# A sparse 3x3 convolution on one core: a fifth pair of images loaded up front in two parts, a wait ahead of the first store, and twelve more matmuls on zeros

## The chip, the core and the metric

The kernel runs on one core of a Trainium2 chip. The core has five engines that run their own instruction streams: TensorE (PE in the profile, with its weight loads shown as PEld), VectorE (DVE), ScalarE (ACT), GpSimd (POOL) and SyncE (SP, which here only issues transfers). Sixteen DMA engines move data between the chip's memory (HBM) and the on-chip buffer (SBUF); matmuls write to the accumulators (PSUM). Engines wait for each other by semaphores.

The metric is the time of one execution on the device in microseconds (us); the median over several executions is given. A profiled execution also leaves a trace, in which the span from the first to the last instruction can be read engine by engine.

## The reference

A batch of 16 images with 64 channels of 64 x 64 is convolved with 128 filters of 3 x 3, padding 1. About 90% of the weights are zero, but the kernel treats them as any others.

```python
batch, c_in, h, w, c_out, k = 16, 64, 64, 64, 128, 3
x_pad = np.pad(x, ((0, 0), (0, 0), (pad, pad), (pad, pad)), mode='constant')
for b in range(batch):
    for co in range(c_out):
        for ci in range(c_in):
            for kh in range(k):
                for kw in range(k):
                    if weight[co, ci, kh, kw] != 0:
                        output[b, co] += weight[co, ci, kh, kw] * x_pad[b, ci, kh:kh+h, kw:kw+w]
```

Input and output are 32-bit floats: 16.8 MB of images are read and 33.6 MB of results are written.

## The kernel before

**Tiling.** Two images form a pair, `p` = 0 to 7. The 64 channels of the first image lie on partitions 0 to 63, those of the second on 64 to 127, in a bf16 tile `xs[p]` of 128 x 64 x 64 (`x0` to `x7`, all eight held at once). A matmul takes 64 partitions, one filter tap and 8 rows of 64 pixels, and the matmuls for the two images of a pair alternate, each on its half of the array. A pair is worked in four blocks of 16 rows.

**Two ways to compute a block.** Only the first block of pair 0 is done by `direct` (L150): nine taps, added up in PSUM, copied out by ScalarE and VectorE. All others are done by `twos` (L157), which saves products by working on two output rows at once: GpSimd adds neighbouring rows into `s` (L160), the products of `s` with the middle filter row are shared by even and odd output rows, ScalarE copies them to `pc` (L167), and VectorE adds `pc` to the products of the even and of the odd rows (L174), writing the output tile `o`. This needs differences of filter rows (`G21`, `G01`, L107), made once at the start.

**Start.** SyncE issues the load of the weights (L60) and of the upper 32 rows of pair 0 in 32-bit form (L62). GpSimd issues the lower half of pair 0 (L63), then the identity matrix for transposing, then the pairs 1 to 3 (L68, `EARLY = 4`). Transfers issued by GpSimd convert to bf16 on the way. They run in queue q0, those of SyncE in queue q1, and both queues are served by the same 16 DMA engines. Meanwhile TensorE runs 27 matmuls on a tile of zeros (L80), whose result nobody reads; then it transposes the three filter rows (L103), with casts before (L97) and copies behind them (L116 to L120). The upper half of pair 0 is cast in three pieces by VectorE and ScalarE (L93), and the products (L141) begin when the first piece is there.

**Order.** The schedule is written by hand (`manual_schedule`): each engine runs its instructions in the order of the program text. SyncE's queue holds the two loads of the start and then only stores: two per pair, each of one whole image (L198, 2 MB), issued once VectorE has written all of it; for the last pair four of 1 MB (L195). GpSimd's queue holds the adds (L160) and, between them, the loads of the later pairs: in pair `p`, block 1, it issues the load of pair `p + 3` (L187, L188), so pair 4 during pair 1. Output tiles come from a pool of seven buffers, of which the head of pair 0 uses one at first.

Of the kernel before, what the change touches and what calls it, by code (L numbers as in the profile page):

```python
# [27 lines left out]
def kernel(  # L28
# [6 lines left out]
    nc = tc.nc  # L35

    B, C_IN, H, W = x.shape
    C_OUT, _, KH, KW = weight.shape
    assert (B, C_IN, H, W) == (16, 64, 64, 64) and (C_OUT, KH, KW) == (128, 3, 3)
    NP = B // 2  # L40
# [14 lines left out]
    def pair(p):  # L55
        return x[2 * p : 2 * p + 2].rearrange("n i h w -> (n i) h w")

    xs = [x_pool.tile([128, H, W], BF16, name=f"x{p}") for p in range(NP)]
# [5 lines left out]
    ident = const_pool.tile([128, 128], BF16, name="ident")  # L64
    make_identity(nc, ident)

    def load(p):
        nc.gpsimd.dma_start(out=xs[p], in_=pair(p))  # L68


    EARLY = 4
    for p in range(1, EARLY):
        load(p)


    idle_rhs = const_pool.tile([128, 128], BF16, name="idle_rhs")
    nc.vector.memset(idle_rhs, 0.0)  # L77
    idle_ps = psum_pool.tile([128, 128], FP32, name="ps")
    for _ in range(27):
        nc.tensor.matmul(idle_ps, idle_rhs, idle_rhs, start=True, stop=True)  # L80

# [8 lines left out]
    def cast_x(copy, a, b):  # L92
        copy(out=xs[0][:, a:b, :], in_=x_head[:, a:b, :])  # L93
# [5 lines left out]
    def transposed(g):  # L99
        wps = psum_pool.tile([128, 4, 128], FP32, name="ps")  # L100
        for j in range(3):
            src = w_bf[:, g, C_IN * j : C_IN * (j + 2)]
            nc.tensor.matmul(wps[:, j, :], src, ident, start=True, stop=True)  # L103
        return wps[:, 0:3, :]

    def difference(g, wps):
        nc.vector.tensor_tensor(out=wT[:, g], in0=wps, in1=wT[:, G1], op=SUB)  # L107
# [10 lines left out]
    nc.vector.tensor_copy(out=wT[:, G0], in_=ps0)  # L118
    ps2 = transposed(G2)
    nc.scalar.copy(out=wT[:, G2], in_=ps2)  # L120
    cast_x(nc.scalar.copy, 9, 18)
    difference(G01, ps0)
    difference(G21, ps2)
# [26 lines left out]
    def direct(p, o, r0, rows):  # L150
        ps = product(
            [(xs[p], G1, r0, 1), (xs[p], G0, r0 - 1, 1), (xs[p], G2, r0 + 1, 1)], rows
        )
        nc.scalar.copy(out=o[0][:, r0 : r0 + rows, :], in_=ps[0])  # L154
        nc.vector.tensor_copy(out=o[1][:, r0 : r0 + rows, :], in_=ps[1])  # L155

    def twos(p, o, r0):  # L157
        t0 = r0 // 2
        s = s_pool.tile([128, 8, W], BF16, name="s")
        nc.gpsimd.tensor_tensor(  # L160
            out=s, in0=xs[p][:, r0 : r0 + 16 : 2, :], in1=xs[p][:, r0 + 1 : r0 + 16 : 2, :], op=ADD
        )
        shared = product([(s, G1, 0, 1)], 8)
        pc = []
        for n in range(2):
            c = p_pool.tile([128, 8, W], FP32, name="pc")
            nc.scalar.copy(out=c, in_=shared[n])  # L167
            pc.append(c)
        even = [(xs[p], G21, r0 + 1, 2), (xs[p], G0, r0 - 1, 2)]
        odd = [(xs[p], G01, r0, 2), (xs[p], G2, r0 + 2, 2)]  # L170
        for first, terms in ((r0, even), (r0 + 1, odd)):
            ps = product(terms, 8)
            for n in range(2):
                nc.vector.tensor_tensor(  # L174
                    out=o[n][:, first : r0 + 16 : 2, :], in0=ps[n], in1=pc[n], op=ADD
                )

    for p in range(NP):
        o = [o_pool.tile([C_OUT, H, W], FP32, name="o") for _ in range(2)]
        last = p == NP - 1  # L180
        for blk in range(4):
            r0 = 16 * blk
            if BLOCKS[p][blk] == "T":
                twos(p, o, r0)


                if p > 0 and blk == 1 and p + EARLY - 1 < NP:  # L187
                    load(p + EARLY - 1)  # L188
            else:
                for r, rows in ((r0, 8), (r0 + 8, 8)):  # L190
                    direct(p, o, r, rows)
            if last and blk % 2 == 1:
                for n in range(2):
                    rows = slice(r0 - 16, r0 + 16)
                    nc.sync.dma_start(out=out[2 * p + n][:, rows, :], in_=o[n][:, rows, :])  # L195
        if not last:
            for n in range(2):
                nc.sync.dma_start(out=out[2 * p + n], in_=o[n])  # L198


# [28 lines left out]
```

## Time and profile before

| what | value |
|---|---|
| median of 6 executions | 127.4 us (127.31 to 131.36) |
| the profiled execution's own time | 127.35 us |
| its span, first to last instruction | 125.5 us |
| TensorE busy | 108.6 us, 87% of the span |
| VectorE busy | 82.3 us, 66% |
| GpSimd busy | 40.6 us, 32% |
| ScalarE busy | 38.9 us, 31% |
| mean granted clock of TensorE | 0.952 of full speed |
| bytes moved, as the DMA engines count them | 42.93 MB, mean 342 GB/s |
| loads of 1 MB in bf16 by GpSimd, issue to landing | 15.6 us in the median |
| stores of 2 MB, issue to landing | 16.5 us in the median |

How to read it: a busy share is an average over the whole span. A transfer's "landing" is the time at which its completion is signalled, so it holds the time behind other transfers in its queue as well as its own. Bytes are counted as they are written: a casting load reads two bytes for each that it counts, so 210 GB/s of such loads and 420 GB/s of stores keep the DMA engines equally busy. The clock column of a window is the share of TensorE's full clock that was granted in it. A window is a stretch of the span in us, and its row gives the busy time of each engine with the number of instructions in brackets, then clock, DMA share and GB/s. "SPq" is SyncE's issuing of a transfer, "POOLq" GpSimd's.

### The profile page before, as it was taken

To read this page: it belongs to the slowest core of one execution; us is meant where nothing else is said; L and a number is where in the kernel's file an instruction comes from. 1 tells how busy PE (TensorE), PEld (TensorE's weight loads), DVE (VectorE), ACT (ScalarE), POOL (GpSimd) and SP (SyncE) were. 2 spreads that over 40 slices of the span, in tenths; PEclk is the share of its full clock that TensorE was granted. 3 is DMA by queue.
4 is the path that set the end of the run, shared out by engine and by line. 5 is a ranking of instruction groups with operands and counts; after the bars stand their busy time and mean duration, and the time that the engine had idled before them with its cause. 6 is when DMAs were issued, how large, how long until landed. Compare 5 with 4: busy or idle time off the path is not lost.

```text
span 125.5 us, 2486 instructions
## 1 busy us (share of the span) xinstructions
PE 108.6 (87%) x1002; PEld 55.8 (44%) x1002; DVE 82.3 (66%) x135; ACT 38.9 (31%) x71; POOL 40.6 (32%) x45
## 2 busy tenths in 40 slices
PE   6539999999999999999999999999999999990000
PEld 6414454554455455545555455545554554540000
DVE  0343278788878877877787778777877787774000
ACT  4541533333333333333333333333333333330000
POOL 6309434333433343334333333333333330000000
PEclk9977999999999999999999999999999999999655
DMA  4999999999999999999999999999999999999990
GB/s 135 348 230 212 217 209 217 214 151 402 444 358 303 319 386 363 319 324 379 379 295 313 379 423 428 439 428 415 433 433 423 433 413 418 428 420 407 426 384 37
DMA packets 4044, 42.93 MB, mean 342 GB/s; under 512 B 448, under 2 KB 448, under 8 KB 704
## 3 DMA queue, kind: packets, MB, share of 16 engines
q1 hardware_dynamic: 2880, 34.90, 66.2%
q0 software_dynamic: 1152, 7.86, 30.9%
q8 instruction: 8, 0.13, 0.4%
q14 instruction: 4, 0.03, 0.1%
HBM read 17.07 MB, written 33.55 MB: 403 GB/s over the span
## 4 chain that ended last, share of the span: by engine, by line
PE 82%; DMA 5%; DVE 1%; issue 1%; DVEq 0%; SPq 0%
PE ps L141 82%; DMA o<-in_x_dram 5%; DVE o L174 1%; DVEq L224 0%; DVE x L93 0%; SPq L60 0%; DVEq L174 0%
## 5 line engine op out<-in xcount | busy, mean ns | idle before, releaser
L141 PE MATMUL ps<-x,wT 64*128 64x504 bf16 (+3 forms) x780 | 89.9, 378 | 3.3 <-DVE x L93 3.3
L174 DVE TENSOR_TENSOR o<-ps,pc 128x512 f32<-128x512 f32 x124 | 77.8, 685 | 22.1 <-PE ps L141 19.8
L141 PEld LDWEIGHTS <-wT 64*128 64x128 bf16 x966 | 52.5, 95 | 55.1 <-issue 4.8
L160 POOL TENSOR_TENSOR s<-x 128x512 bf16<-128x512 bf16 x31 | 35.6, 1150 | 60.4 <-PE ps L141 43.1
L167 ACT COPY pc<-ps 128x512 f32<-128x512 f32 x62 | 33.3, 589 | 64.0 <-issue 61.8
L141 PE MATMUL ps<-s,wT 64*128 64x512 bf16 (+1 forms) x186 | 25.5, 377 | 0.0
L80 PE MATMUL ps<-idle_rhs 128*128 128x128 bf16 x27 | 3.1, 313 | 1.0 <-DVE idle_rhs L77 1.0
L68 POOL DMA_DIRECT2D x<-in_x_dram x7 | 3.9, 559 | 0.0
L155 DVE COPY o<-ps 128x512 f32<-128x512 f32 x2 | 1.4, 692 | 3.3 <-PE ps L141 3.3
L80 PEld LDWEIGHTS <-idle_rhs 128*128 128x128 bf16 x27 | 2.8, 148 | 1.0 <-DVE idle_rhs L77 1.0
L97 DVE CAST w_bf<-w_sb 128x192 bf16<-128x192 f32 (+1 forms) x4 | 1.1, 352 | 2.7 <-DMA w_sb<-in_weight_dram 2.7
L93 DVE CAST x<-o 128x576 bf16<-128x576 f32 x1 | 0.5, 460 | 3.1 <-DMA o<-in_x_dram 3.1
L154 ACT COPY o<-ps 128x512 f32<-128x512 f32 x2 | 1.2, 585 | 3.8 <-PE ps L141 3.8
L93 ACT CAST x<-o 128x576 bf16<-128x576 f32 (+1 forms) x2 | 1.5, 803 | 2.3 <-DMA o<-in_x_dram 2.3
L97 ACT ACT_TABLE_LOAD x1 | 1.3, 1283 | 0.7 <-PEq L213 0.7
L97 ACT CAST w_bf<-w_sb 128x64 bf16<-128x64 f32 (+1 forms) x2 | 0.7, 417 | 1.6 <-DMA w_sb<-in_weight_dram 1.6
L103 PE MATMUL ps<-ident,w_bf 128*128 128x128 bf16 x9 | 0.9, 232 | 0.1
L107 DVE TENSOR_TENSOR wT<-ps,wT 128x384 bf16<-128x384 f32 x2 | 1.0, 547 | 0.0
L63 POOL DMA_DIRECT2D x<-in_x_dram x1 | 0.7, 691 | 0.8 <-POOLq L213 0.8
L103 PEld LDWEIGHTS <-w_bf 128*128 128x128 bf16 x9 | 0.6, 104 | 0.6 <-DVE w_bf L97 0.6
L77 DVE MEMSET idle_rhs<- 128x64 uint32 x1 | 0.1, 112 | 0.8 <-PEq L213 0.8
L116 ACT CAST wT<-ps 128x384 bf16<-128x384 f32 x1 | 0.5, 478 | 0.2 <-PE ps L103 0.2
(8 smaller groups left out, 1.9 us busy)
## 6 DMA issues: line engine op xcount, KB each, us to landing
out_dram<-o SPq DMA_DIRECT2D x14, 2048.0 KB, 16.5
x<-in_x_dram POOLq DMA_DIRECT2D x7, 1024.0 KB, 15.6
out_dram<-o SPq DMA_DIRECT2D x4, 1024.0 KB, 9.8
o<-in_x_dram SPq DMA_DIRECT2D x1, 1024.0 KB, 6.7
x<-in_x_dram POOLq DMA_DIRECT2D x1, 512.0 KB, 7.8
w_sb<-in_weight_dram SPq DMA_DIRECT2D x1, 288.0 KB, 2.9
```

The lines of the kernel that those rows point to most:

```text
L68: nc.gpsimd.dma_start(out=xs[p], in_=pair(p))
L80: nc.tensor.matmul(idle_ps, idle_rhs, idle_rhs, start=True, stop=True)
L93: copy(out=xs[0][:, a:b, :], in_=x_head[:, a:b, :])
L97: copy(out=w_bf4[:, g, a:b, :], in_=w_v[:, k : k + b - a, :])
L103: nc.tensor.matmul(wps[:, j, :], src, ident, start=True, stop=True)
L107: nc.vector.tensor_tensor(out=wT[:, g], in0=wps, in1=wT[:, G1], op=SUB)
L141: nc.tensor.matmul(ps[n][:, lo:hi, c_lo:c_hi], tap(g, kw, n), src[q, a:b:step, c_lo + kw - 1 : c_hi + kw - 1], start=(i == 0), stop=(i == ...
L154: nc.scalar.copy(out=o[0][:, r0 : r0 + rows, :], in_=ps[0])
L155: nc.vector.tensor_copy(out=o[1][:, r0 : r0 + rows, :], in_=ps[1])
L160: nc.gpsimd.tensor_tensor(out=s, in0=xs[p][:, r0 : r0 + 16 : 2, :], in1=xs[p][:, r0 + 1 : r0 + 16 : 2, :], op=ADD)
L167: nc.scalar.copy(out=c, in_=shared[n])
L174: nc.vector.tensor_tensor(out=o[n][:, first : r0 + 16 : 2, :], in0=ps[n], in1=pc[n], op=ADD)
```

## The change

Three things change. Line numbers are those of the kernel before, unless said.

- `EARLY` becomes 5, and `load` takes a range of rows. Pairs 1 to 3 are loaded up front as before; pair 4 now too, as two transfers, rows 0 to 35 and rows 36 to 63. The first of the two is remembered as `landed`. The condition in the loop is moved along with it: the loads of pairs 5, 6 and 7 are issued at the places where they were (in pairs 2, 3 and 4, block 1), and the one of pair 4 is gone from pair 1.
- The first store of the kernel (pair 0, first image) gets one more wait: for `landed`.
- Twelve more matmuls on zeros come right after the transposes of the third filter row, ahead of the first product.

```diff
-    def load(p):
-        nc.gpsimd.dma_start(out=xs[p], in_=pair(p))
-    EARLY = 4
-    for p in range(1, EARLY):
+    def load(p, a=0, b=H):
+        return nc.gpsimd.dma_start(out=xs[p][:, a:b, :], in_=pair(p)[:, a:b, :])
+    EARLY = 5
+    for p in range(1, EARLY - 1):
         load(p)
+    landed = load(EARLY - 1, 0, 36)
+    load(EARLY - 1, 36, H)
...
-    for _ in range(27):
-        nc.tensor.matmul(idle_ps, idle_rhs, idle_rhs, start=True, stop=True)
+    def keep_busy(n):
+        for _ in range(n):
+            nc.tensor.matmul(idle_ps, idle_rhs, idle_rhs, start=True, stop=True)
+    keep_busy(27)
...
     ps2 = transposed(G2)
     nc.scalar.copy(out=wT[:, G2], in_=ps2)
+    keep_busy(12)
...
-                if p > 0 and blk == 1 and p + EARLY - 1 < NP:
-                    load(p + EARLY - 1)
+                if p > 1 and blk == 1 and p + EARLY - 2 < NP:
+                    load(p + EARLY - 2)
...
-                nc.sync.dma_start(out=out[2 * p + n], in_=o[n])
+                st = nc.sync.dma_start(out=out[2 * p + n], in_=o[n])
+                if p == n == 0:
+                    tc.add_manual_dep(
+                        st.ins,
+                        landed.ins.name,
+                        mybir.DependencyInfo(
+                            mybir.DependencyClass.Sync, mybir.DependencyReason.DATA
+                        ),
+                        reason="loads first",
+                    )
```

In the order of each engine this gives: GpSimd issues six loads before its first add instead of four, and one fewer among the adds of pair 1; SyncE's instructions keep their order, with the wait ahead of the third transfer; TensorE has 24 more instructions (12 weight loads, 12 matmuls) between the transposes and the first product; VectorE and ScalarE are as before.

## The prediction

> **What bounds the kernel now.** I read the page first, then the chain of waits, then SyncE's own waits, and last the trace by windows. From the page:
>
> ```profile
> span 125.5 us, 2486 instructions
> PE 108.6 (87%) x1002; PEld 55.8 (44%) x1002; DVE 82.3 (66%) x135; ACT 38.9 (31%) x71; POOL 40.6 (32%) x45
> DMA  4999999999999999999999999999999999999990
> ...
> q1 hardware_dynamic: 2880, 34.90, 66.2%
> q0 software_dynamic: 1152, 7.86, 30.9%
> ...
> out_dram<-o SPq DMA_DIRECT2D x4, 1024.0 KB, 9.8
> ```
>
> The DMA engines are full from the second slice to the last but one; their two queues (q1 is SyncE's: weights, head of x, all stores; q0 is GpSimd's: the casting loads) add to 97% of the span. The chain of waits names PE for 82%, but look where it ends:
>
> ```profile
> 8.39 103.43 PE ps L141 x954
> ...
> 113.17 0.60 DVEq L224
> 113.77 0.60 DVE o L174
> ```
>
> ```profile
> SPq L224 <- DMA out_dram<-o: 8.7, 4, 2.4
> ```
>
> Compute is over at 114.37 us, and SyncE then waits 8.7 us for four stores, one after another at up to 2.4 us. A last store of 1 MB lands 9.8 us after its issue although 2.4 us of engine time would move it: it queues behind earlier stores. So the end is set by a backlog of transfers. The end of the span by windows (us, clock, DMA share, GB/s):
>
> ```profile
> 114.00:120.00 6.00, 0.00 (x0) 0.00 (x0) 0.36 (x1) 0.00 (x0) 0.00 (x0) 0.75 1.01 423
> ...
> 121.00:122.00 1.00, 0.00 (x0) 0.00 (x0) 0.00 (x0) 0.00 (x0) 0.00 (x0) 0.50 0.86 360
> 122.00:123.00 1.00, 0.00 (x0) 0.00 (x0) 0.00 (x0) 0.00 (x0) 0.00 (x0) 0.50 0.43 180
> 123.00:124.00 1.00, 0.00 (x0) 0.00 (x0) 0.00 (x0) 0.00 (x0) 0.00 (x0) 0.50 0.08 33
> ```
>
> The 16 engines run dry between about 121.6 and 123.9: the slowest of them sets the time. Hence the rule for this case: only lost DMA time counts. There is one conspicuous loss, at the first store, issued at 24.21:
>
> ```profile
> 20.00:24.00 4.00, 4.00 (x40) 2.05 (x38) 3.27 (x6) 1.07 (x2) 1.15 (x1) 1.00 1.06 221
> ...
> 25.00:26.00 1.00, 1.00 (x14) 0.52 (x10) 0.68 (x2) 0.15 (x1) 0.33 (x1) 1.00 1.23 229
> 26.00:27.00 1.00, 1.00 (x13) 0.46 (x11) 1.00 (x3) 0.00 (x0) 0.00 (x0) 1.00 1.17 131
> 27.00:28.00 1.00, 1.00 (x12) 0.54 (x10) 0.83 (x2) 0.77 (x2) 0.68 (x1) 1.00 0.82 106
> 28.00:29.00 1.00, 1.00 (x14) 0.49 (x10) 0.44 (x1) 0.31 (x1) 0.47 (x1) 1.00 0.86 311
> ```
>
> From 25 to 28 the engines are busy, but the bytes fall by half. The DMA view of these 3 us lists q0 alone: 57 packets at 107.3% of 16 engines, that is 51.5 engine-us, 0.90 us a packet; between 24 and 25 it lists 23 packets at 89.9%, 0.625 us each. At 0.625, the 57 would have taken 35.6. Lost: 15.9 engine-us, 1.0 us on each engine (by bytes: 466 KB against 3 x 221, 0.9 us). The slowing begins about 1.1 us after SyncE issued the two stores of pair 0; not one q1 packet is listed before 28.3.
>
> **The change part by part.** The sum is made against the profiled execution: span 125.5, time 127.35 with 1.85 around it; the median of the runs is 127.4.
>
> *Fifth pair earlier, in two parts.* GpSimd issues x4 at 18.87 now and would at about 4.1, behind the three loads that start at 2.46 and take 0.54 each. The queue is in order, and the third of these lands only at 23.74 (issued 3.54, 20.2 to landing), so x4's bytes move when they moved before: no gain by itself. Cost: one more issue, 0.57 us; two now stand before GpSimd's first add at 9.47, in an idle stretch of 5.4 us ("ACT x L93", its cast, is what that add waits for). Without that cover it would be 1.1 us on GpSimd, itself 32% busy. The later loads keep their places (sixth pair in the third pair's block 1, and so on). Nine loads instead of eight: a load more in the same bytes; smaller packets (9 and 7 KB of source instead of 16) show no loss here, since 8 KB packets of the first pair took 0.32 us against 0.62.
>
> *Twelve more matmuls on zeros.* The 27 take 3.06 us, so 12 take 1.36, from 5.1 to 6.5, in the gap that ends at 8.39 with x's first cast. PE idles there by 3.28 us, so 1.9 stays over; if x came 1.9 earlier they would start to cost. Nothing is queued behind them but products that wait for that cast. The granted clock tells what they may bring:
>
> ```profile
> 5.10:7.70 2.60, 0.01 (x1) 1.00 1.05 241
> 7.70:8.35 0.65, 0.00 (x0) 0.52 1.42 290
> 8.35:11.10 2.75, 2.71 (x14) 0.50 1.02 213
> ```
>
> (us, PE busy, clock, DMA share, GB/s.) The clock halves 2.6 us after PE went idle, and the first 2.75 us of products run at half. With only 1.9 us idle it may stay up: products done up to 1.37 us earlier, and so everything behind them on VectorE. On the time this is worth zero: each later store is issued 1.4 us earlier into a queue that is 7 us behind. If the clock drops all the same, also zero.
>
> *First store waits for the first part.* The three whole loads land at 13.96, 19.02 and 23.74, 4.9 us apart. 36 of 64 rows are 2.75 us: the first part lands at 26.5, the store is issued at 26.55 instead of 24.21 (22.8, had PE the warm clock and no wait), 2.3 us later. Behind it in SyncE's queue are the second store of pair 0 and then those of pair 1, at 36.95 now, 10 us off. Output buffers come free later by as much: the first to be reused has its store landed at 36.6 and is written again at about 50, so 11 us remain. The rest of x4, 28 rows, takes 2.15 us more; undisturbed, the last engine has it at 28.3 (it ended the load before at 23.4, the first at 22.3: that is where the 16 completion packets fall) and the first at 27.2.
>
> Now the unknown, L: time from a store's issue to its first packet. Rows: the weights, issued on the same queue at 0.74 with idle engines, have their first packet at 1.74, L = 1.0; the first store, issued at 24.21 with engines full, has it at 28.32, L = 4.1. I take the nearer to 1.0, because x4's queue is running empty by then and in the row with 4.1 the store's packets start just when q0 has run out on most engines. With L = 1.0, stores start at 27.55: the earliest engines idle up to 0.35 us, 0.1 on the mean, the late ones never. And the slow stretch, which began 1.1 us after the issue, would begin at 27.65, with hardly a load packet left to slow. So: -1.0 (slow packets) + 0.1 (idle) = -0.9 us.
>
> Bounds: by the packet records of the trace, the two late engines had two slow packets each (0.7 and 1.8 us; 1.0 and 1.6) where 0.62 is usual, which cost them 1.3 us, and it is they that matter at the end: -1.3. At L = 4.1, stores start at 30.65, the mean engine idles 2.9 and wins 1.0: +1.9; the slowest idles 2.35 and wins 1.3: +1.0. The end is between: about +1.0, as early engines have some 2 us of slack at the end.
>
> Two rules of the Trainium skill speak against this part. "DMA: Bandwidth & Descriptors", section on queues, rings and completion order, has each engine go round-robin between the queues it has work for, packet by packet. By it, stores issued at 24.21 would have shared the engines from 25.2 on, and holding them back only reorders the same bytes: sum 0, 127.4. The rows of 25 to 28 do not show that: q0 alone, and slow. The same page's rules for kernel authors say to issue a DMA early and wait late; by that, a store held back 2.3 us costs up to 2.3, 129.7. The rows answer that the engines have 3 to 4 us of loads queued at 24.2 anyway. I go by the rows.
>
> **Rivals.**
> 1. *The slow stretch moves along.* If it belongs to starting SyncE's empty queue while GpSimd's is running, it comes again on x4's second part, or as a slower start of the stores. For it: two parts leave 2.15 us of load running at the issue. Against: by the spacing, most of that is gone 1.1 us after. It gives back the 1.0: 127.35 - 1.0 + 1.0 + 0.1 = 127.45, no change. That the change does nothing measurable otherwise (the stretch was of this one execution) falls in here.
> 2. *Slower: the engines stand empty between loads and stores.* Place: after x4's second part; price as above, L minus 1.75 us of cover on the slowest engine (26.55 to 28.3) minus 1.3. It decides from L = 3.05 on; at 4.1 it costs 1.0: 128.4. For it: 4.1 is the only row for a store. Against: that row has full engines, and weights needed 1.0.
> 3. *PE becomes worth something*: if stores fell behind compute no more, 1.37 us of clock would show, 126.0 or less. Against: 8.7 us of landing waits at the end.
>
> **How the numbers follow.** Forecast, -0.6 to -1.3 us: 0.46; time 127.35 - 0.9 = 126.45. Rival 1: 0.27. Rival 2: 0.24. Rival 3 and better: 0.03. A measurement of this kernel tells about 0.5%, 0.64 us, from no change; so the forecast and rival 3 are mostly faster (a little of the forecast falls short): 0.47; rival 1 and the mild part of rival 2: 0.28; slower: 0.25. The forecast's own range is 126.0 to 126.8. The range of 8 in 10 takes in rival 1 and most of rival 2: 125.9 to 128.4.
>
> **What would show it.** Right: GB/s of about 220 through 25 to 27.5 and above 400 by 29; first store issued near 26.5; first q1 packets within 1.5 us of it; clock 1.00 through 8 to 11; the slowest engine dry near 123. Wrong: a second with a DMA share under 0.6 between 27 and 31 (rival 2); q0 packets over 0.9 us again after the issue, or first stores of over 0.62 us (rival 1). The prediction falls altogether if the backlog at the end isn't there, that is if the last store lands within some 4 us of its issue.

## The result, and the profile after

The changed kernel takes 128.21 us in the median (127.6 to 129.51, 21 runs), the one before 127.42 (47 runs); the ratio of the two is 1.0061, 95% interval 1.0046 to 1.0076. It is slower by 0.8 us, where 0.9 us less was forecast. Here and below, medians and ranges are over all executions, while ratios leave out some executions that fell into a slower state. The profiled execution took 128.48 us with a span of 126.6.

From the page of the changed kernel, and SyncE's own waits (who waited for whom: us in total, times, longest):

```profile
span 126.6 us, 2511 instructions
...
DMA  4999999999999999999999999999999999999980
...
out_dram<-o SPq DMA_DIRECT2D x4, 1024.0 KB, 11.3
...
x<-in_x_dram POOLq DMA_DIRECT2D x1, 576.0 KB, 23.5
```

```profile
SPq L206 <- DMA x<-in_x_dram: 26.0, 1, 26.0
...
SPq L241 <- DMA out_dram<-o: 10.3, 4, 3.0
```

The engines are still full, and the last stores queue even longer (11.3 us to landing instead of 9.8). The first store now waits for a load, as meant: the first part of the fifth pair, issued at 4.05, lands 23.5 us later at 27.54, and the timeline has the store right behind it:

```profile
27.63 2.56 SPq L206 DMA_DIRECT2D out_dram<-o  x2
```

The windows of the changed kernel (us, engines, clock, DMA share, GB/s) where the stores start, where the sixth pair's load comes in, and at the end:

```profile
25.00:26.00 1.00, 1.00 (x14) 0.50 (x10) 1.00 (x2) 0.00 (x0) 0.00 (x0) 1.00 1.06 211
26.00:27.00 1.00, 1.00 (x12) 0.48 (x10) 1.00 (x3) 0.17 (x1) 0.08 (x1) 1.00 1.04 207
27.00:28.00 1.00, 1.00 (x12) 0.55 (x10) 0.42 (x1) 0.90 (x2) 1.00 (x1) 1.00 0.89 176
28.00:29.00 1.00, 1.00 (x14) 0.47 (x10) 0.85 (x2) 0.00 (x0) 0.07 (x1) 1.00 0.70 264
...
35.00:36.00 1.00, 1.00 (x12) 0.55 (x10) 1.00 (x3) 0.00 (x0) 0.00 (x0) 1.00 0.90 279
36.00:37.00 1.00, 1.00 (x12) 0.55 (x10) 1.00 (x2) 0.53 (x2) 0.43 (x1) 1.00 1.15 262
37.00:38.00 1.00, 1.00 (x14) 0.55 (x10) 0.40 (x2) 0.54 (x2) 0.72 (x1) 1.00 0.91 254
...
122.00:123.00 1.00, 0.00 (x0) 0.00 (x0) 0.00 (x0) 0.00 (x0) 0.00 (x0) 0.50 0.74 311
123.00:124.00 1.00, 0.00 (x0) 0.00 (x0) 0.00 (x0) 0.00 (x0) 0.00 (x0) 0.50 0.31 131
124.00:125.00 1.00, 0.00 (x0) 0.00 (x0) 0.00 (x0) 0.00 (x0) 0.00 (x0) 0.50 0.06 25
```

Here is the kernel before from 35 to 37, where its sixth pair's load joins the stores:

```profile
35.00:36.00 1.00, 1.00 (x13) 0.54 (x11) 0.96 (x2) 0.00 (x0) 0.00 (x0) 1.00 1.15 442
36.00:37.00 1.00, 1.00 (x12) 0.53 (x10) 1.00 (x3) 0.12 (x1) 0.02 (x1) 1.00 1.01 319
```

Three things are to be seen. The two slow rows, 26 and 27, are gone: 207 and 176 GB/s where there were 131 and 106 from 26 to 28. Instead the share falls to 0.70 from 28 to 29: the engines stand empty. And from 35 to 37 they are busy but move 279 and 262 GB/s, where the kernel before moved 442 and 319. That last stretch is new.

To compare traces I value each packet record at its usual duration (611 ns for 16 KB on the 32-bit side), add up over the 16 engines, and take a sixteenth of it from the time elapsed. What is left is DMA time lost per engine, whether the engines were empty or their packets slow. Two traces before, three of the changed kernel (the further ones come from experiments below):

```
                        22.5-25  25-29  29-33  33-38.5   in all up to 112 us
before                    0.0     1.0    0.0     0.0      3.55
before, second trace      0.0     0.8    0.0     0.0      3.49
changed                   0.3     0.5    0.1     0.8      4.46
changed, second trace     0.1     0.6    0.1     0.9      4.25
changed, third trace      0.0     0.3    0.1     0.9      4.12
```

The changed kernel loses 4.28 us on the mean of three, the one before 3.52: 0.76 us more. Some 2.5 us of each sum lie ahead of 22 us. This counts the mean engine. The last engine ends 1.4 and 1.6 us after the mean one in the two traces before, 1.7, 1.7 and 1.95 in the three of the changed kernel, 0.3 more. Together that is 1.0 us, and these profiled executions are 0.97 us apart (127.35 and 127.31; 128.48, 128.16 and 128.26); the medians are 0.8 apart.

### The profile page after: what moved, and what is told of

Read it like the earlier page. It is cut to its first block, busy times and chain, and to the rows that moved or that the text cites. A ratio compares the mean times of both kernels' runs of the same rounds, so it can differ in the third digit from the quotient of the medians.

```text
span 126.6 us, 2511 instructions
## 1 busy us (share of the span) xinstructions
PE 109.4 (86%) x1014; PEld 57.3 (45%) x1014; DVE 82.3 (65%) x135; ACT 38.9 (31%) x71; POOL 41.1 (32%) x46
## 4 chain that ended last, share of the span: by engine, by line
PE 82%; DMA 5%; DVE 1%; issue 1%; DVEq 0%; SPq 0%
PE ps L149 82%; DMA o<-in_x_dram 5%; DVE o L182 1%; DVEq L241 0%; DVE x L100 0%; SPq L60 0%; DVEq L182 0%
## 5 line engine op out<-in xcount | busy, mean ns | idle before, releaser
L149 PEld LDWEIGHTS <-wT 64*128 64x128 bf16 x966 | 53.4, 95 | 53.1 <-issue 3.7
L168 POOL TENSOR_TENSOR s<-x 128x512 bf16<-128x512 bf16 x31 | 35.6, 1151 | 59.5 <-PE ps L149 42.2
L85 PE MATMUL ps<-idle_rhs 128*128 128x128 bf16 x39 | 3.9, 282 | 1.0 <-DVE idle_rhs L80 1.0
L68 POOL DMA_DIRECT2D x<-in_x_dram x8 | 4.4, 559 | 0.0
L85 PEld LDWEIGHTS <-idle_rhs 128*128 128x128 bf16 x39 | 3.5, 130 | 1.0 <-DVE idle_rhs L80 1.0
L63 POOL DMA_DIRECT2D x<-in_x_dram x1 | 0.7, 691 | 0.8 <-POOLq L230 0.8
L125 DVE CAST wT<-ps 128x384 bf16<-128x384 f32 x1 | 0.6, 552 | 0.0
## 6 DMA issues: line engine op xcount, KB each, us to landing
out_dram<-o SPq DMA_DIRECT2D x4, 1024.0 KB, 11.3
x<-in_x_dram POOLq DMA_DIRECT2D x1, 576.0 KB, 23.5
```

The source lines that it names most:

```text
L68: return nc.gpsimd.dma_start(out=xs[p][:, a:b, :], in_=pair(p)[:, a:b, :])
L149: nc.tensor.matmul(ps[n][:, lo:hi, c_lo:c_hi], tap(g, kw, n), src[q, a:b:step, c_lo + kw - 1 : c_hi + kw - 1], start=(i == 0), stop=(i == ...
L168: nc.gpsimd.tensor_tensor(out=s, in0=xs[p][:, r0 : r0 + 16 : 2, :], in1=xs[p][:, r0 + 1 : r0 + 16 : 2, :], op=ADD)
```

## The experiments

Theory A said that the wait leaves the engines empty for half a us and that this is the whole loss; B, that a slow stretch of about 1 us comes in every run, at one place or another, and the wait adds its gap; C, that the earlier, split loads cost by themselves.

**No wait (e1).** The changed kernel without the dependency of the first store.

```diff
-                if p == n == 0:
-                    tc.add_manual_dep(st.ins, landed.ins.name, ...)
```

> The changed kernel without the wait ahead of the first store; loads and zeros as in the change. Theory A (the wait leaves the DMA engines empty for about half a us between the loads and the first stores, and that is the whole loss): first store issued near 23.8 us, no second between 27 and 31 with a DMA share under 0.8, time back at 127.4 or below (126.9 to 127.5). Theory B (a slow stretch of about 1 us comes in every run, wherever a queue starts beside a running one; the wait adds its gap on top): the same 127.4, but with slow load packets at 25 to 28 as before the change. Theory C (the split, earlier loads cost by themselves, by an engine that falls behind early): 127.9 to 128.2, the wait being worth nothing.

Measured: 127.7 us, ratio to before 1.0014 (0.9988 to 1.0040). Its trace has the slow loads back, at 26 to 28:

```profile
26.00:27.00 1.00, 1.00 (x13) 0.51 (x10) 1.00 (x2) 0.00 (x0) 0.00 (x0) 1.00 1.05 137
27.00:28.00 1.00, 1.00 (x13) 0.45 (x11) 1.00 (x3) 0.20 (x1) 0.11 (x1) 1.00 0.94 160
```

and no loss at 33 to 38. So it is the wait that costs, at least most of the 0.8 us; C falls, and B fits better than A.

**No additional matmuls (e2), and these alone (e3).**

```diff
-    keep_busy(12)
```

> The changed kernel without the twelve additional matmuls; wait and loads as in the change. Theories A and B: 128.2 (127.9 to 128.4), as the end is set by a backlog of stores and TensorE has nothing to do with it. Rival: the twelve matmuls or their fetching disturb the start; then 127.4 to 127.7.

> The kernel before with only the twelve additional matmuls. Theories A and B: 127.4 (127.2 to 127.6); the clock before the first products still falls to 0.50 for some 3 us, as it did in the changed kernel. Rival (the matmuls disturb the start): 127.8 or more.

Measured: e2 128.23 us, ratio 1.0059 (1.0035 to 1.0083), as slow as the full change. e3 127.53 us, ratio 0.9975 (0.9955 to 0.9994): at most half a per cent faster. TensorE is not what made the kernel slower. e2's trace is of one of its fastest executions (127.74 us): it has the stretch (0.8 us lost at 33 to 38.5) but a gap of only 0.2, and loses 0.2 us more in all than the kernel before. Whether the twelve keep the clock up differs from run to run. The rows of 8.35 to 11.10 (us, PE, clock, DMA share, GB/s) in the first trace of the changed kernel:

```profile
8.35:11.10 2.75, 2.75 (x17) 0.52 1.06 222
```

and in the second:

```profile
8.35:11.10 2.75, 2.75 (x28) 1.00 1.01 212
```

The clock was half in the one and full in the other; their times, 128.48 and 128.16, stand on the same side of 127.4.

**A shorter first part (e4).** Rows 0 to 15 instead of 0 to 35, so that 48 rows cover the store's way.

```diff
-    landed = load(EARLY - 1, 0, 36)
-    load(EARLY - 1, 36, H)
+    landed = load(EARLY - 1, 0, 16)
+    load(EARLY - 1, 16, H)
```

> The changed kernel with the first part of the fifth pair cut to rows 0 to 15, so that it lands some 1.5 us earlier and more load is left to cover the first store's way to the engines. Theory A: first store issued near 25 to 26 us, no idle engines before the first store packets, and the time falls by the gap of 0.5 to 0.8 us: 127.4 or, if the slow load packets stay away, 126.5 to 127.0. Theory B: the gap is gone but a slow stretch of about 1 us is there, beside the rest of the load or later: 127.4 to 127.6. Theory C: 128.0 to 128.3.

Measured: 127.6 us, ratio 1.0003 (0.9981 to 1.0024). No engine stands empty (0.0 us lost from 27 to 29), and nothing is won either. The first part's small packets are slow already at 23 to 25, before any store is issued (the store comes at 26.73), and the sixth pair's load loses 0.2 at 33 to 38.5:

```profile
23.00:25.00 2.00, 2.00 (x23) 1.06 (x20) 1.71 (x3) 0.12 (x1) 0.30 (x1) 1.00 1.06 144
```

B is right in the sum, 0.1 to 0.2 us apart from before; why it comes at 23 here, this run doesn't tell.

**Second traces (e5, e6)** of both kernels, unchanged, to see whether the place of the slow stretch is chance. Theory G is A's gap; J says that the slow stretch belongs to the first time that one queue starts among packets of the other; R, that its place is random.

> The kernel before, once more, for a second trace. So far the traces without the wait lose about 1 us of DMA time at 25 to 28 us, those with the wait lose 0.1 to 0.3 at 23 to 25 and 0.8 at 34 to 37.5. Theory J (the stretch belongs to the first time that one DMA queue starts among the packets of the other): slow load packets at 25 to 28 again, 0.8 to 1.1 us lost, and nothing at 34 to 38. Theory R (it comes at a random place in each execution): some other place.

> The changed kernel, once more, for a second trace. Theory J: no loss of packets at 25 to 28, idle engines for 0.1 to 0.6 us near 28, slow packets at 34 to 37.5 where the sixth pair's load joins the stores, 0.7 to 0.9 us lost there. Theory R: the slow stretch elsewhere.

Measured, one execution each: 127.31 and 128.16 us. The kernel before, second trace:

```profile
26.00:27.00 1.00, 1.00 (x14) 0.51 (x10) 1.00 (x3) 0.03 (x1) 0.00 (x0) 1.00 1.37 180
27.00:28.00 1.00, 1.00 (x12) 0.52 (x10) 0.57 (x1) 1.00 (x2) 0.94 (x1) 1.00 0.76 123
...
35.00:36.00 1.00, 1.00 (x14) 0.57 (x12) 1.00 (x3) 0.00 (x0) 0.00 (x0) 1.00 1.15 418
```

The changed kernel, second trace:

```profile
27.00:28.00 1.00, 1.00 (x12) 0.51 (x10) 1.00 (x3) 0.00 (x0) 0.00 (x0) 1.00 0.79 160
...
34.00:35.00 1.00, 1.00 (x12) 0.56 (x10) 1.00 (x3) 0.12 (x1) 0.02 (x1) 1.00 1.22 279
35.00:36.00 1.00, 1.00 (x14) 0.57 (x10) 0.53 (x1) 0.96 (x2) 1.00 (x1) 1.00 0.47 115
```

The places repeat, so R falls. The changed kernel's stretch came 1.3 us earlier than in the first trace, and the sixth pair's load was issued 1.6 us earlier (at 29.67 instead of 31.26).

**The sixth pair's load two blocks later (e7).**

```diff
-                if p > 1 and blk == 1 and p + EARLY - 2 < NP:
+                if p > 1 and blk == 3 and p + EARLY - 2 < NP:
```

> The changed kernel with the loads of the sixth to eighth pair issued two blocks later (block 3 instead of block 1), some 6.4 us. Theory J: the slow packets move with the load that joins the stores, from 35-37.5 to about 41-44 us; time unchanged at 128.0 to 128.4. Theory R, or a theory that ties the stretch to the end of a pair of images (the second stores, near 36): still at 34 to 37.5, or anywhere.

Measured: 127.54 us, ratio 1.0005 (0.9979 to 1.0031). The load is issued at 35.80, and the stretch has gone with it:

```profile
36.00:37.00 1.00, 1.00 (x12) 0.57 (x10) 1.00 (x2) 0.00 (x0) 0.37 (x1) 1.00 1.24 524
37.00:38.00 1.00, 1.00 (x14) 0.50 (x10) 1.00 (x3) 0.24 (x1) 0.14 (x1) 1.00 1.00 410
...
40.00:41.00 1.00, 1.00 (x14) 0.49 (x10) 1.00 (x3) 0.00 (x0) 0.00 (x0) 1.00 1.12 262
41.00:42.00 1.00, 1.00 (x12) 0.55 (x10) 0.60 (x2) 0.99 (x2) 0.90 (x1) 1.00 0.77 180
```

0.06 us are lost from 33 to 38.5 and 0.82 from 38.5 to 43. So the stretch belongs to the load that joins the stores, and not to a place in the schedule. The time was a miss for J: 128.0 was expected.

**Waiting for the whole pair (e8)**, the suspected gap made larger.

```diff
-    landed = load(EARLY - 1, 0, 36)
-    load(EARLY - 1, 36, H)
+    load(EARLY - 1, 0, 36)
+    landed = load(EARLY - 1, 36, H)
```

> The changed kernel with the first store waiting for the second part too, so that no load is left to cover its way to the engines. Theory G (idle engines between loads and stores are what the change lost, about half a us): store issued near 29 to 30, engines empty for about 2 us more (0.9 to 1.0 us for the way of a store, plus the wait for the slowest engine), the time 129.2 to 130.5. If the gap doesn't count (other engines' slack takes it): 128.2 to 128.6.

Measured: 130.34 us, ratio 1.0234 (1.0200 to 1.0268). The store is issued at 29.38, and a whole microsecond passes without a byte:

```profile
28.00:29.00 1.00, 1.00 (x12) 0.57 (x10) 0.84 (x2) 0.76 (x2) 0.66 (x1) 1.00 0.16 29
29.00:30.00 1.00, 1.00 (x14) 0.51 (x10) 0.44 (x1) 0.32 (x1) 1.00 (x2) 1.00 0.00 0
```

2.3 us are lost from 27 to 33, against 0.4 to 0.6 with the 36 rows, and the time is 2.1 us above the changed kernel's. Empty engines are paid in full.

**All loads up front (e9: with the wait, e10: without).** All x tiles have their own memory, so every load can run ahead of the stores, and then no load meets them later.

```diff
-    EARLY = 5
+    EARLY = 8
...
-    landed = load(EARLY - 1, 0, 36)
-    load(EARLY - 1, 36, H)
+    landed = load(EARLY - 1, 0, 16)
+    load(EARLY - 1, 16, H)
```

> The changed kernel with all seven remaining pairs loaded up front, the last in two parts (rows 0 to 15, then 16 to 63), the first store waiting for the first of these. Every store then runs after the loads, so that no queue starts among full packets of the other, save at the hand-over, where 3.7 us of load cover the store's way. Theories J and G together: first store near 40 to 42 us, no slow stretch of 0.8 us anywhere after 5 us, the time 126.4 to 126.9, better than both kernels. If the slow stretch comes anyway (at the hand-over, or tied to something else): 127.3 to 127.6. If output buffers run out in the third or fourth pair and then TensorE ends later than the stores' backlog covers: 128 or more.

> The same with all loads up front but without the wait: the first stores start among the loads at 24 to 25 us. Theory J: slow packets at 25 to 28, about 0.9 us lost, then none; the time 127.2 to 127.6, like the kernel before. If the difference to the run with the wait is under 0.3 us, the stretch isn't what the wait saves there.

Measured: e9 127.78 us, ratio 1.0031 (1.0017 to 1.0045); e10 127.3 us, ratio 0.9992 (0.9977 to 1.0007). e10 bears J out: slow packets at 25 to 29 (1.0 us lost), and none later, although loads and stores run side by side until 66 us:

```profile
26.00:27.00 1.00, 1.00 (x12) 0.51 (x10) 1.00 (x2) 0.38 (x1) 0.29 (x1) 1.00 0.98 123
27.00:28.00 1.00, 1.00 (x12) 0.55 (x10) 0.27 (x2) 0.70 (x2) 0.86 (x1) 1.00 0.99 147
...
36.00:37.00 1.00, 1.00 (x12) 0.55 (x10) 0.91 (x2) 0.73 (x2) 0.63 (x1) 1.00 1.05 328
```

In e9 only 0.5 us are lost, from 33 to 43 us (the small packets of the last pair's first part), and up to 112 us it has lost 3.40, less than any other trace. But it is not faster. Its end:

```profile
121.00:122.00 1.00, 0.00 (x0) 0.00 (x0) 0.00 (x0) 0.00 (x0) 0.00 (x0) 0.50 0.64 270
122.00:123.00 1.00, 0.00 (x0) 0.00 (x0) 0.00 (x0) 0.00 (x0) 0.00 (x0) 0.50 0.31 131
123.00:124.00 1.00, 0.00 (x0) 0.00 (x0) 0.00 (x0) 0.00 (x0) 0.00 (x0) 0.50 0.06 25
124.00:125.00 1.00, 0.00 (x0) 0.00 (x0) 0.00 (x0) 0.00 (x0) 0.00 (x0) 0.50 0.02 8
```

By the completion packets, 15 engines are through at 123.01 and the last at 124.46; the mean engine ends at 122.24, the last 2.2 us after it (1.4 to 1.6 before the change). A share of 0.06 and 0.02 is one engine at work. The forecast of 126.4 to 126.9 missed for two reasons: the small packets took back 0.5 us of what the absent stretch saved, and the forecast counted the mean engine, while the last one fell 0.7 us further behind it.

**The pair e6 and e7 once more, timed side by side (e11, e12).**

> The changed kernel, timed on the same chip and in the same rounds as the next run. Theories J and G: 128.0 to 128.3, ratio to before 1.004 to 1.008.

> The changed kernel with the loads of the sixth to eighth pair two blocks later, once more. Up to the store's start nothing differs from the run beside it, and the slow stretch has only moved, so by theories J and G it must be as slow: 127.9 to 128.3. The earlier run of it gave 127.54. If it is again 0.4 to 0.7 us below the run beside it, the time at which the next load joins the stores costs something besides the slow stretch (by the engines that it leaves behind), and J and G do not account for the whole loss.

Measured on one chip: the changed kernel 128.23 us, ratio 1.0058 (1.0034 to 1.0081); with the later loads 127.67, ratio 1.0014 (1.0000 to 1.0028). e12 loses 4.27 us up to 112, as much as the changed kernel, 0.82 of it from 38.5 to 43; but its last engine ends 1.4 us after the mean one, in e7 1.5, against 1.7, 1.7 and 1.95 in the three traces of the changed kernel. So the later loads give back 0.5 us although the slow stretch and, in e12, the gap (0.7 us lost at 25 to 29) are still there: some 0.5 of the 0.8 us hang on when the later loads come. In e12's trace the difference stands at the spread of the engines; e7's also lost 0.3 us less, about half of it by a smaller gap. More than that isn't shown: the spread is read from single executions, and it is 2.0 us in the trace of e3, where only zeros were added, and 1.9 in e10, which has no wait, but 1.3 in e1. I have no experiment that sets the spread by itself.

## Why the prediction was wrong, point by point

- **What bounds the kernel: right.** Lost DMA time is what counts, on the engine that ends last: the mean engine's losses (+0.76 us) and the last one's distance from it (+0.3) add up to the difference of the traced executions; a whole us of empty engines more (e8) is paid as such; a clock that is up or not doesn't show.
- **Fifth pair earlier, in two parts, at no price: right.** Without the wait the kernel is at 1.0014 (0.9988 to 1.0040) of the time before, so the price is 0.4% at most.
- **Twelve matmuls worth zero: right, nearly** (e2 against the full change: 1.0059 and 1.0061; alone, in e3, they are worth 0.25%). The clock may stay up, as the prediction put it, and does so in some runs only.
- **"With L = 1.0, stores start at 27.55": the way was right, its start was not.** From issue to first packet it took 0.85 us (27.63 to 28.48). But the store was issued at 27.63, 27.45 and 27.30 in the three traces, not at 26.55. A landing is the landing on the slowest engine: in the first trace 15 engines had the first part by 26.15, and the last at 27.28. I had taken the last engine from a trace in which the last two were only 0.5 us behind the rest. So the engines stood empty for 0.3 to 0.5 us instead of 0.1.
- **"-1.0 (slow packets)": this is the step that failed.** The time was saved at 25 to 28 and spent again 8 us later. The slow stretch was read as a price of issuing the store at 24.2; the runs show that it comes the first time that loads and stores run together, whichever comes second (e4 apart, see the end). Held back, the stores ran alone, and the sixth pair's load became the one that joins: 0.8 to 0.9 us, by 36 in the changed kernel, by 41 when that load was moved (e7, e12), and still by 27 where nothing waits (e1, e10). Put into the prediction's sum, +0.85 for the stretch and 0.3 more for the gap turn -0.9 into about +0.3. What remains is in these traces the last engine's distance from the mean (0.3 us), which the sum, made for the mean engine, did not have, the small packets at 23 to 25 (0.1) and smaller losses. Why the last engine falls behind, and why later loads (e7, e12) bring the time back to within 0.2% of before, stays open.
- **Rivals.** The first named the mechanism ("the slow stretch moves along") and looked for it in the wrong place, on the fifth pair's second part, at a price of no change. The second named the place of the gap, but as a matter of L, which was 0.85. Neither put the two together: a stretch that moves and a gap that stays is a loss.
- **The signs.** Of the signs of being wrong, none came where they were looked for: no second from 27 to 31 had a share under 0.6 (the lowest was 0.70), and neither loads nor first stores were slow, but for single packets. Of those of being right, the bytes from 25 to 27 and the first store packets within 1.5 us of the issue came, and the time was lost all the same, at 35 to 37, where no sign was set.

The trace of before could have warned: the fifth pair's load was not the last to run beside stores; the sixth pair's began beside them at 35.6 without loss, after the slow stretch at 25 to 28 was over.

The Trainium skill, "DMA: Bandwidth & Descriptors", section on queues, rings and completion order, has the engines take turns between their queues, packet by packet; the traces agree for the later meetings (in the changed kernel 64 packets of q0 and 77 of q1 from 39 to 44 us, with 0.1 us lost from 38.5 to 43), but not for the first (2 of q0 and 15 of q1 from 36 to 37).

## What to carry to other kernels

Where a backlog of transfers sets the end, a wait on a load costs what the slowest engine adds to that load's landing, and it must be covered by work that is still queued, not by its mean. Before booking a slow stretch as saved, look which transfer will be the next to meet the condition that made it slow. And add up the losses for the engine that ends last, since a mean that falls (e9) need not shorten anything.

No version beats both kernels by more than half a per cent: the twelve matmuls alone come out at 0.9975 (0.9955 to 0.9994) of the time before, all loads up front without a wait at 0.9992 (0.9977 to 1.0007).

## What the runs showed of the hardware that was not expected

- **The first meeting of loads and stores.** Packets of the queue already running take about twice as long for some two us, and hardly any of the new queue's move. In the DMA view of the changed kernel, from 36 to 37 us:

```profile
q1 hardware_dynamic: 15, 0.25, 107.3%
q0 software_dynamic: 2, 0.02, 7.8%
```

15 packets of 16 KB in 17.2 engine-us (107.3% of 16) are 1.14 us each, where 0.61 is usual. It came in every trace but e4 and e9 with 0.8 to 1.1 us lost per engine, and at no later meeting. In both of these the first stores start just as the loads run out. In e9 no load comes after them; in e4 the sixth pair's load joins them with only 0.2 us lost, an exception that is not explained. Nor is it the first meeting of the two queues in any sense: GpSimd's first load joins SyncE's load of the head at 5.2 us, and under 0.1 us is lost from 5 to 7 in the first traces of both kernels. What the engines do in the slow stretch was not found.
- **A GpSimd load's first effect comes 4 us after its issue**: the slow packets begin 4.0 to 4.1 us after the sixth pair's issue in the first trace of the changed kernel (31.26, 35.3) and in e7 (35.80, 39.9). The Trainium skill, same page, section on latency and other measured facts, gives about 1 us to the first byte of a load issued by GpSimd and 0.6 us for a transfer of SyncE's; here SyncE's store needed 0.85.
- **One engine falls behind early.** In the three traces of the changed kernel one engine ends the third pair's load 0.9 to 1.3 us after the next, and a 16 KB instruction fetch of 0.94 to 0.97 us stands in the packet records a few us before it (13.7 to 15.4 us). That the fetch is the cause was not tested, and the traces before speak against it as the whole cause: they have the same fetch at 16.0 and 16.8 us, and the last engine ends that load 0.1 and 0.2 us after the next.
- **Small casting packets were slow** at the start of a first part of 16 rows, 0.7 us lost in e4 and 0.5 in e9, and up to 0.3 with 36 rows, without any other queue starting. Not explained.
